# A product-key retrieval kernel: half of each chunk's second-table rows split into rounded halves, and the expert choice dealt out in finer steps

## The chip, the cores and the metric

The kernel runs on one core of a Trainium2 chip. The metric is the device time of one execution in microseconds. A core has five engines with a queue of instructions each: TensorE (PE, matmuls), VectorE (DVE), ScalarE (ACT), GpSimd (POOL) and SyncE (SP). An engine takes its instructions strictly in order and waits at one until what it needs has been signalled.

## The reference

One layer of a diffusion backbone over 640 tokens (128 context, 512 latent). The part that matters here is the channel mixer at its end, a retrieval over 16384 experts, each a row `u` of one table and a row `v` of another, both 2048 wide:

```python
top, sel = lax.top_k(cand, PEER_TOPK)          # 8 heads, 16 experts a head and token
idx = jnp.take_along_axis(cidx, sel, axis=-1)
g = jax.nn.softmax(top, axis=-1)
def block(args):                               # a block of 128 tokens
    xc, ic, gc = args
    act = jnp.einsum("cd,ckd->ck", xc, u_tab[ic])
    w = gc * jax.nn.gelu(act)
    return jnp.einsum("ck,ckd->cd", w, v_tab[ic])
```

`cand` are the sums of the 16 best scores of two key halves of 128 keys, so three kinds of top-16 are taken for each token and head.

## The kernel before

All stages up to the scores of the experts (modulation, mixers, projections) end about 2557 us into the span and are not touched. The rest is the function `experts`. It goes through five blocks of 128 tokens in the order 3, 4, 2, 1, 0. For each block a list of the experts that any of its tokens chose exists in HBM, and the block runs over this list in chunks of 256 experts. The first 24 chunks of a block (`K0`) are unconditional; further ones stand in nested `If`s on the length of the list.

A chunk (function `chunk`) fetches its 256 rows of `u` as two gathers of 128 rows, 1 MB each (`gather_u`, into `ur`), and turns them on TensorE in eight **turns** (`turn(g)`: four transposes of 128x128 into one of two PSUM tiles `tb`, a rounded copy `uh` by ScalarE, and the remainder `ul` by VectorE, whose row is named `wl<-tb,wh`). `up(g)` multiplies: three rounded (fp32r) products for each of two 128-blocks, xh*uh, xh*ul, xl*uh, into `a`. After `up(7)` ScalarE takes the GELU. The second half of a chunk's work is done while the next chunk turns, and the next chunk's code calls it `pending`: `up(7)`, then `weigh` (the GELU's result is transposed into a `tb` tile and multiplied by the gathered gates `gr` into `w`), then eight **downs** (`down(u)`, u = 4j + d: `w[:, j]` times 512 columns of `vr[j]`, in full fp32, summed into `acc[:, d]`). So one chunk's code is: turn 0, up 7 of before, turn 1, weigh, up 0, then for g = 2 to 7 turn g, down g-2, up g-1, and at the end downs 6 and 7.

The gathers are indirect DMAs that GpSimd issues, in the order in which the code calls them: the two halves of the next chunk's `u`, the gates (`gather_g`, two), two small gathers of list entries (`entries`), and the two halves of this chunk's `v` rows (`gather_v`, `vr[0]` after down 3, `vr[1]` after down 7 of before, since they overwrite what those read).

While a block runs, the experts of the next block are chosen (`choose`, a generator that `experts` steps once after each of the nine `yield`s of a chunk), mostly on VectorE: `top16` over 16 score rows of 128, sums `cand`, `top16` over 8 rows of 256, one-hot sums, then 32 rounds that build the gate table `Gs` by one-hot matmuls (`oh`, `dd`), and the list. The end of the block before (`finish`: gate, residual, layer norm, output) is a second generator, which is stepped at every other yield from chunk 1 on. The order of each engine's instructions in this stage is pinned to the order of the code (`pin`).

Of the kernel before, what the change touches and what calls it, by code (L numbers as in the profile page):

```python
# [7 lines left out]
F32 = mybir.dt.float32  # L8
F32R = mybir.dt.float32r
# [27 lines left out]
NCH = 64  # L37
# [114 lines left out]
class Kern:  # L152
# [871 lines left out]
                self.nc.vector.scalar_tensor_tensor(x[:, s], x[:, s], a, g, op0=o0, op1=o1)  # L1024

    def top16(self, vals, idx, src):
        v = self.nc.vector
        v.max(vals[:, 0:8], src)
        v.max_index(idx[:, 0:8], vals[:, 0:8], src)
        v.match_replace(src, vals[:, 0:8], src, -3.0e38)  # L1030
        v.max(vals[:, 8:16], src)
        v.max_index(idx[:, 8:16], vals[:, 8:16], src)

    def choose(self, b, S=None):
# [8 lines left out]
        IX = T.tile([128, 16, 16], U32, name="IX", tag="IX", bufs=1)  # L1043
        for c in range(16):
            self.top16(V[:, c], IX[:, c], S[:, c])
            if c % 2:
                yield
        IF = T.tile([128, 16, 16], F32, name="IF", tag="IF", bufs=1)
        v.tensor_copy(IF, IX)
        sh = [128, 8, 16, 16]  # L1050
# [3 lines left out]
        cand = T.tile(sh, F32, name="cand", tag="Gs", bufs=1)  # L1054
# [4 lines left out]
        TV = T.tile([128, 8, 16], F32, name="TV", tag="TV", bufs=1)  # L1059
        SE = T.tile([128, 8, 16], U32, name="SE", tag="SE", bufs=1)  # L1060
        for h in range(8):
            self.top16(TV[:, h], SE[:, h], cand[:, h].rearrange("p a b -> p (a b)"))
            yield

        I12 = T.tile([128, 3, 128], F32, name="I12", tag="I12", bufs=1)
# [36 lines left out]
        for n in range(34):  # L1102
            if full is not None:
                n1, p = full
                if n1 % 8 == 0:
                    st = T.tile([128, 128, 32], F32, name="Gs", tag="Gs", bufs=1)
                nc.scalar.copy(st[:, :, n1 % 8 * 4:n1 % 8 * 4 + 4], p.rearrange("j t i -> j i t"))
                if n1 % 8 == 7:
                    nc.sync.dma_start(self.G_d[b][:NE].rearrange("(i j) t -> j i t", j=128)
                                      [:, :, n1 // 8 * 32:n1 // 8 * 32 + 32], st)  # L1110
            full = None
            if ready is not None:
                n1, oh, dd = ready
                p = ps.tile([128, 4, 128], F32, name="g", tag="m", bufs=1)
                for j in range(4):
                    nc.tensor.matmul(p[:, j], oh[:, j], dd[:, j], start=True, stop=True)  # L1116
                full = n1, p
            ready = None
            if n < 32:
                oh = T.tile([128, 4, 128], F32, name="oh", tag="oa", bufs=2)  # L1120
                dd = T.tile([128, 4, 128], F32, name="dd", tag="od", bufs=2)
                for j in range(4):
                    k1, k2, w = (it[:, i, n * 4 + j:n * 4 + j + 1] for i in range(3))
                    v.tensor_scalar(oh[:, j], self.iota, k2, None, op0=ALU.is_equal)
                    v.tensor_scalar(dd[:, j], self.iota, k1, w, op0=ALU.is_equal, op1=ALU.mult)
                    if j == 1:
                        yield
                ready = n, oh, dd
            yield
            if n % 8 == 1 and n > 1:  # L1130
                for q in range(4):
                    v.tensor_reduce(cnt[:, n // 8 - 1, q * 32:q * 32 + 32], st[:, q * 32:q * 32 + 32], axis=AX.X,
                                    op=ALU.add)
                    yield

                for _ in range(20 if n < 32 else 0):
                    yield

        f = T.tile([128, 128], F32, name="f", tag="f", bufs=1)
        v.tensor_reduce(f, cnt.rearrange("p q i -> p i q"), axis=AX.X, op=ALU.add)  # L1140
# [7 lines left out]
        for r in range(16):  # L1148
            s = slice(r * 8, r * 8 + 8)
            v.max(L[:, s], f)  # L1150
            if r < 15:
                v.match_replace(f, L[:, s], f, 0.0)
            if r % 4 == 3:
                yield
        li = T.tile([128, 128], I32, name="li", tag="li", bufs=1)
        v.tensor_scalar(li, L, -1.0, None, op0=ALU.add)
# [86 lines left out]
    def up(self, g, x):  # L1243
# [5 lines left out]
        if g == 7:  # L1249
            self.nc.scalar.activation(self.t, self.a, AF.Gelu_apprx_tanh)  # L1250

    def weigh(self):

        p = self.bank()[:, :256].rearrange("p (j t) -> p j t", j=2)
        for j in range(2):
            self.nc.tensor.transpose(p[:, j], self.t[:, j * 128:j * 128 + 128], self.ident)  # L1256
        self.nc.vector.tensor_mul(self.w, p, self.gr)  # L1257

    def down(self, u, first):

        j, d = divmod(u, 4)
        self.nc.tensor.matmul(self.acc[:, d], self.w[:, j], self.vr[j][:, d * 512:d * 512 + 512],  # L1262
                              start=first and j == 0, stop=j == 1, skip_group_check=True)

    def chunk(self, i, c, pending, rows=None):


        nc, b = self.nc, self.order[i]
        self.nbank = 1
        x = self.xs[i % 2]  # L1270
        rows = rows or self.ur[c % 2]
        if c + 1 < NCH:
            self.gather_u(b, c + 1, 0)
        self.turn(0, rows)
        if pending is not None:
            first, before = pending
            self.up(7, before)
        self.turn(1, rows)
        yield
        if pending is not None:  # L1280
            self.weigh()
        self.gather_g(b, c)
        if c + 3 < NCH:
            self.entries(b, c + 3)
        self.up(0, x)
        yield
        if c + 1 < NCH:
            self.gather_u(b, c + 1, 1)
        for g in range(2, 8):
            self.turn(g, rows)  # L1290
            if pending is not None:
                self.down(g - 2, first)
                if g - 2 == 3:
                    self.gather_v(b, c, 0)
            self.up(g - 1, x)
            yield
        if pending is not None:
            self.down(6, first)
            self.down(7, first)
        else:  # L1300
            self.gather_v(b, c, 0)
        self.gather_v(b, c, 1)
        yield

# [69 lines left out]
    def experts(self):  # L1374
# [7 lines left out]
        self.ur = [[one([128, D], "ur%d%d" % (c, j)) for j in range(2)] for c in range(2)]  # L1382
        hb = self.H[GB]
        self.xs = [[t[:, j] for t in hb] for j in range(2)]
        first = [one([128, D], "uf%d" % j) for j in range(2)]
        pieces = [[t[:, k * 512:k * 512 + 512]
                   for t in [self.wp.tile([128, 1024], F32R, name=n, tag=n, bufs=self.hl_bufs) for _ in range(3)]
# [13 lines left out]
        for i, b in enumerate(self.order):  # L1401
            more = self.choose(self.order[i + 1]) if i < 4 else iter(())
            for c in range(K0):
                if c == 0 and i:
                    fin = self.finish(i - 1)
                    next(fin)
                for n, _ in enumerate(self.chunk(i, c, pending, rows)):
                    next(more, None)
                    if c and n % 2:
                        next(fin, None)  # L1410
                if c == 0:
                    next(fin, None)
                rows, pending = None, (c == 0, self.xs[i % 2])
                if c == 0 and i < 4:
                    self.load_x(i + 1)
            for _ in more:
                pass
            if i < 4:
                rows = first
# [13 lines left out]
            mark = self.pin()  # L1433
        self.nbank = 1
        self.up(7, pending[1])
        self.weigh()
        for u in range(8):
            self.down(u, False)
# [99 lines left out]
```

## Time and profile before

| what | us |
|---|---|
| median of 3 runs (5272.74 to 5280.17) | 5276.44 |
| the profiled execution's own time | 5268.44 |
| its span, first to last instruction | 5266.7 |

The profile is of one execution. Its times count from the span's start, so "at 4868.02" is a place in the program, and the 1.7 us between the span and that execution's own time lie around the program. The median of the timed runs is 8.0 us above the profiled execution.

### The profile page before, as it was taken

To read this page: it belongs to the slowest core of one execution; us is meant where nothing else is said; L and a number is where in the kernel's file an instruction comes from. 1 tells how busy PE (TensorE), PEld (TensorE's weight loads), DVE (VectorE), ACT (ScalarE), POOL (GpSimd) and SP (SyncE) were. 2 spreads that over 40 slices of the span, in tenths; PEclk is the share of its full clock that TensorE was granted. 3 is DMA by queue.
4 is the path that set the end of the run, shared out by engine and by line. 5 is a ranking of instruction groups with operands and counts; after the bars stand their busy time and mean duration, and the time that the engine had idled before them with its cause. 6 is when DMAs were issued, how large, how long until landed. Compare 5 with 4: busy or idle time off the path is not lost. (4 is left out here: it accounts for less than half of the span.)

```text
span 5266.7 us, 74372 instructions
## 1 busy us (share of the span) xinstructions
PE 4800.3 (91%) x29015; PEld 3989.4 (76%) x29015; DVE 2879.7 (55%) x6240; ACT 1599.6 (30%) x2561; POOL 1601.8 (30%) x1628
## 2 busy tenths in 40 slices
PE   8999989999999997969699979997999889989997
PEld 3799879999999977759577657765677667767775
DVE  6693593466534544781555566555655484634333
ACT  3324424433223123323133223322332223323222
POOL 2000493000000004534243434343334434344442
PEclk8999989999999998989799999999999999999998
DMA  6544336554325465563578768776777668867765
GB/s 238 195 173 144 126 129 213 192 173 172 114 98 165 147 214 200 158 153 136 187 242 257 233 221 272 244 235 240 254 242 243 255 218 267 247 231 290 260 250 212
DMA packets 576711, 1085.00 MB, mean 206 GB/s; under 512 B 375643, under 2 KB 388955, under 8 KB 501819
## 3 DMA queue, kind: packets, MB, share of 16 engines
q0 software_dynamic: 97712, 596.41, 30.5%
q1 hardware_dynamic: 460394, 429.32, 27.4%
q10 hardware_dynamic: 18208, 54.08, 2.6%
q8 instruction: 239, 3.92, 0.3%
q14 instruction: 158, 1.29, 0.1%
HBM read 967.53 MB, written 112.13 MB: 205 GB/s over the span
## 5 line engine op out<-in xcount | busy, mean ns | idle before, releaser
L1241 DVE TENSOR_TENSOR wl<-tb,wh 128x512 fp32r<-128x512 f32 x1072 | 738.0, 690 | 1368.1 <-ACT wh L1240 1366.7
L1240 ACT CAST wh<-tb 128x512 fp32r<-128x512 f32 x1072 | 627.5, 585 | 1873.2 <-PE tb L1239 1776.6
L1262 PE MATMUL acc<-vr,w 128*128 128x512 f32 x2144 | 1096.8, 604 | 30.3 <-DVE w L1257 30.1
L1248 PE MATMUL a<-wh,hh 128*128 128x256 f32 x2144 | 966.9, 451 | 1.8 <-PEq L1426 1.8
L1239 PE MATMUL tb<-cst,ur 128*128 128x128 f32 x4160 | 649.6, 279 | 68.1 <-DMA ur<-in_pu,ix 58.1
L1248 PE MATMUL a<-wl,hh 128*128 128x256 f32 x2144 | 618.8, 289 | 48.9 <-DVE wl L1241 48.7
L193 ACT CAST wh<-wr 128x1024 fp32r<-128x1024 f32 x339 | 355.5, 1050 | 983.4 <-PE a L630 380.4
L1248 PE MATMUL a<-wh,hl 128*128 128x256 f32 x2144 | 614.2, 286 | 0.0
L1248 PEld LDWEIGHTS a<-wl,hh 128*128 128x128 f32 x2144 | 419.9, 196 | 255.3 <-issue 170.5
L1239 PEld LDWEIGHTS tb<-cst,ur 128*128 128x128 f32 x4160 | 493.1, 143 | 150.9 <-issue 75.8
L1248 PEld LDWEIGHTS a<-wh,hh 128*128 128x128 f32 x2144 | 420.4, 196 | 199.4 <-issue 189.7
L630 PE MATMUL a<-h,wl 128*128 128x320 f32 x2368 | 550.9, 313 | 19.4 <-DVE wl L194 19.4
L1204 POOL DMA_INDIRECT vr<-in_pv,ix x268 | 256.1, 955 | 1015.5 <-PE acc L1262 909.8
L194 DVE TENSOR_TENSOR wl<-wr,wh 128x1024 fp32r<-128x1024 f32 x281 | 343.8, 1225 | 380.3 <-ACT wh L193 373.6
L630 PE MATMUL a<-h,wh 128*128 128x320 f32 x2368 | 549.0, 313 | 0.0
L630 PE MATMUL a<-l,wh 128*128 128x320 f32 x2368 | 545.9, 312 | 0.0
L1262 PEld LDWEIGHTS acc<-vr,w 128*128 128x128 f32 x2144 | 341.4, 194 | 103.9 <-issue 69.2
L630 PEld LDWEIGHTS a<-h,wl 128*128 128x128 f32 x2368 | 400.9, 190 | 21.7 <-DVE wl L194 21.0
L1248 PEld LDWEIGHTS a<-wh,hl 128*128 128x128 f32 x2144 | 416.2, 194 | 0.0
L630 PEld LDWEIGHTS a<-h,wh 128*128 128x128 f32 x2368 | 405.6, 190 | 12.0
L630 PEld LDWEIGHTS a<-l,wh 128*128 128x128 f32 x2368 | 400.9, 190 | 0.8
L1204 POOL DMA_INDIRECT gr<-G_d,ix x268 | 265.9, 992 | 365.4 <-DVE w L1257 280.9
(396 smaller groups left out, 7450.0 us busy)
## 6 DMA issues: line engine op xcount, KB each, us to landing
wr<-in_wmod SPq DMA_DIRECT2D x152, 512.0 KB
wr<-in_win SPq DMA_DIRECT2D x83, 512.0 KB
G_d<-Gs SPq DMA_DIRECT2D x20, 2048.0 KB
wrx<-in_win SPq DMA_DIRECT2D x69, 512.0 KB
wrx<-in_wmod SPq DMA_DIRECT2D x40, 512.0 KB
wr<-in_wo SPq DMA_DIRECT2D x36, 512.0 KB
wr<-in_wq SPq DMA_DIRECT2D x32, 512.0 KB
wrx<-in_wq SPq DMA_DIRECT2D x32, 512.0 KB
```

The lines of the kernel that those rows point to most:

```text
L193: nc.scalar.copy(h, raw)
L194: (eng or nc.vector).tensor_sub(l, raw, h.bitcast(F32))
L630: nc.tensor.matmul(a, w, x[:, kt, c0:c0 + n], start=kt == 0 and i == 0, stop=kt == nk - 1 and i == 2)
L1204: self.nc.gpsimd.indirect_dma_start(out=out, out_offset=None, in_=table, in_offset=bass.IndirectOffsetOnAxis(ap=idx, axis=0))
L1239: nc.tensor.transpose(p[:, k, j * 128:j * 128 + 128], rows[j][:, kt * 128:(kt + 1) * 128], self.ident)
L1240: nc.scalar.copy(self.uh[g % 4], p)
L1241: nc.vector.tensor_sub(self.ul[g % 4], p, self.uh[g % 4].bitcast(F32))
L1248: self.nc.tensor.matmul(self.a, a[:, kt], w[:, k], start=kt + n == 0, stop=kt == 15 and n == 2)
L1262: self.nc.tensor.matmul(self.acc[:, d], self.w[:, j], self.vr[j][:, d * 512:d * 512 + 512], start=first and j == 0, stop=j == 1, skip_grou ...
```

## The change

1. `down` for the first 128 experts of a chunk (j = 0) is no longer one fp32 product for each d but three rounded ones: Wh*vh, Wh*vl, Wl*vh. The downs of the second 128 experts stay as they are.
2. For this `vr[0]` is split in four pieces of 512 columns: `cast_v(d)` on ScalarE makes the rounded part `vh`, `rest_v(d)` on GpSimd subtracts it and makes `vl`. Pieces 0 and 1 stand in the first step of the next chunk (piece 0 ahead of up 7), pieces 2 and 3 with turns 2 and 3. `weigh` also makes `Wh` (ScalarE) and `Wl` (VectorE) from `w[:, 0]`.
3. The gathers move: both halves of the next chunk's `u` are called in the chunk's first step; the gates, the entries and `vr[0]` with turn 4; `vr[1]` stays at the end.
4. `choose` yields more often in its top-16 parts (16 and 16 steps in place of 8 and 8) and in the list (8 in place of 4); its 20 empty steps after every eighth round become 13, marked "idle". `finish` is stepped only when the choice is idle or over.

```diff
     def top16_steps(self, vals, idx, src):
         v = self.nc.vector
         v.max(vals[:, 0:8], src)
         v.max_index(idx[:, 0:8], vals[:, 0:8], src)
         v.match_replace(src, vals[:, 0:8], src, -3.0e38)
+        yield
         v.max(vals[:, 8:16], src)
         v.max_index(idx[:, 8:16], vals[:, 8:16], src)
...
         for c in range(16):
             self.top16(V[:, c], IX[:, c], S[:, c])
-            if c % 2:
-                yield
+            yield
...
-                for _ in range(20 if n < 32 else 0):
-                    yield
+                for _ in range(13 if n < 32 else 0):
+                    yield "idle"
...
+    def cast_v(self, d):
+
+        s = slice(d * 512, d * 512 + 512)
+        self.nc.scalar.copy(self.vh[:, s], self.vr[0][:, s])
+
+    def rest_v(self, d):
+        s = slice(d * 512, d * 512 + 512)
+        self.nc.gpsimd.tensor_sub(self.vl[:, s], self.vr[0][:, s], self.vh[:, s].bitcast(F32))
...
         self.nc.vector.tensor_mul(self.w, p, self.gr)
+        self.nc.scalar.copy(self.Wh, self.w[:, 0])
+        self.nc.vector.tensor_sub(self.Wl, self.w[:, 0], self.Wh.bitcast(F32))
...
-        self.nc.tensor.matmul(self.acc[:, d], self.w[:, j], self.vr[j][:, d * 512:d * 512 + 512],
-                              start=first and j == 0, stop=j == 1, skip_group_check=True)
+        s = slice(d * 512, d * 512 + 512)
+        for n, (w, x) in enumerate(((self.w[:, 1], self.vr[1][:, s]),) if j else
+                                   ((self.Wh, self.vh[:, s]), (self.Wh, self.vl[:, s]), (self.Wl, self.vh[:, s]))):
+            self.nc.tensor.matmul(self.acc[:, d], w, x, start=first and j == n == 0, stop=j == 1,
+                                  skip_group_check=True)
...
         if c + 1 < NCH:
             self.gather_u(b, c + 1, 0)
         self.turn(0, rows)
-        if pending is not None:
-            first, before = pending
+        if more:
+            self.cast_v(0)
+            self.rest_v(0)
             self.up(7, before)
...
         for g in range(2, 8):
             self.turn(g, rows)
-            if pending is not None:
+            if more:
+                if g < 4:
+                    self.cast_v(g)
+                    self.rest_v(g)
                 self.down(g - 2, first)
-                if g - 2 == 3:
-                    self.gather_v(b, c, 0)
+            if g == 4:
+                self.gather_g(b, c)
+                if c + 3 < NCH:
+                    self.entries(b, c + 3)
+                self.gather_v(b, c, 0)
             self.up(g - 1, x)
             yield
...
                 for n, _ in enumerate(self.chunk(i, c, pending, rows)):
-                    next(more, None)
-                    if c and n % 2:
+                    if next(more, "idle") == "idle" and c:
                         next(fin, None)
```

How the queues stand, first GpSimd's of one chunk (from the second half of a chunk's `v` rows on, in the first block). Before:

```order
L1204 DMA vr_22720<-in_pv,ix 128x2048
L1204 DMA ur_22725<-in_pu,ix 128x2048
L1204 DMA gr<-G_d_17687,ix 128x128 x2
L1204 DMA ix<-L_d_17692,si 128x1 x2
L1204 DMA ur_22726<-in_pu,ix 128x2048
L1204 DMA vr_22719<-in_pv,ix 128x2048
```

The same stretch with the change, where `hl` is the tile that `vl` lies in and `hh` that of `vh`:

```order
L1208 DMA vr_22720<-in_pv,ix 128x2048
L1208 DMA ur_22725<-in_pu,ix 128x2048
L1263 TENSOR_TENSOR hl<-vr_22719,hh 128x512
L1208 DMA ur_22726<-in_pu,ix 128x2048
L1263 TENSOR_TENSOR hl<-vr_22719,hh 128x512 x3
L1208 DMA gr<-G_d_17687,ix 128x128 x2
L1208 DMA ix<-L_d_17692,si 128x1 x2
L1208 DMA vr_22719<-in_pv,ix 128x2048
```

Four subtractions came in, the second `u` gather moved ahead of the four small gathers, and the gather of `vr[0]` now stands behind all of them.

ScalarE's queue from the casts of the last turn and turn 0 (`x2`) to those of turns 2 and 3, before:

```order
L1240 CAST wh<-tb_22743 128x512 x2
L1250 ACTIVATE t<-a 128x256
L1240 CAST wh<-tb_22744 128x512 x2
L1240 CAST wh<-tb_22743 128x512
L1240 CAST wh<-tb_22744 128x512
```

And with the change (`hh<-vr` is `cast_v`, `ACTIVATE t<-a` the GELU):

```order
L1244 CAST wh<-tb_22745 128x512 x2
L1259 CAST hh<-vr_22719 128x512
L1254 ACTIVATE t<-a 128x256
L1244 CAST wh<-tb_22746 128x512
L1259 CAST hh<-vr_22719 128x512
L1271 CAST Wh<-w 128x128
L1244 CAST wh<-tb_22746 128x512
L1259 CAST hh<-vr_22719 128x512
L1244 CAST wh<-tb_22745 128x512
L1259 CAST hh<-vr_22719 128x512
```

The first `cast_v` stands ahead of the GELU, and `Wh` ahead of the cast of turn 2.

VectorE's queue in the first steps of a choice, before: between two remainders `wl` of turns stand two whole top-16s.

```order
L1241 TENSOR_TENSOR wl<-tb_22744,wh 128x512
L1028 MAX V<-S 128x8
L1029 MAX_INDEX IX<-V,S 128x8
L1030 MATCH_REPLACE S<-V,S 128x128
L1031 MAX V<-S 128x8
L1032 MAX_INDEX IX<-V,S 128x8
L1028 MAX V<-S 128x8
L1029 MAX_INDEX IX<-V,S 128x8
L1030 MATCH_REPLACE S<-V,S 128x128
L1031 MAX V<-S 128x8
L1032 MAX_INDEX IX<-V,S 128x8
```

With the change, from the remainder of turn 1 over `weigh` to that of turn 2:

```order
L1245 TENSOR_TENSOR wl<-tb_22746,wh 128x512
L1032 MAX V<-S 128x8
L1033 MAX_INDEX IX<-V,S 128x8
L1034 MATCH_REPLACE S<-V,S 128x128
L1036 MAX V<-S 128x8
L1037 MAX_INDEX IX<-V,S 128x8
L1270 TENSOR_TENSOR w<-tb_22745,gr 128x256
L1272 TENSOR_TENSOR Wl<-w,Wh 128x128
L1032 MAX V<-S 128x8
L1033 MAX_INDEX IX<-V,S 128x8
L1034 MATCH_REPLACE S<-V,S 128x128
L1036 MAX V<-S 128x8
```

One top-16 stands in a step, and `Wl`, which waits for ScalarE's `Wh`, stands behind `w`.

## Rows read from the trace of the kernel before

**Rows 1.** The page's costliest groups, the downs' line (count | busy, mean ns).

```profile
L1262 PE MATMUL acc<-vr,w 128*128 128x512 f32 x2144 | 1096.8, 604 | 30.3 <-DVE w L1257 30.1 <-DMA vr<-in_pv,ix 0.2
```

**Rows 2.** Windows: stretch, its length, each engine's busy time, granted clock, DMA share, GB/s.

```profile
2557.50:4723.80 2166.30, 1944.61 (x11350) 1471.64 (x11350) 1249.37 (x3213) 617.16 (x1106) 841.30 (x868) 0.96 0.73 242
4723.80:5266.70 542.90, 497.50 (x2866) 366.93 (x2866) 198.93 (x316) 151.37 (x267) 221.16 (x232) 0.97 0.68 250
3091.40:3200.80 109.40, 80.35 (x404) 57.59 (x403) 98.62 (x289) 25.55 (x42) 35.46 (x33) 0.88 0.59 207
4802.00:5193.70 391.70, 383.62 (x2254) 285.37 (x2255) 134.84 (x207) 116.57 (x208) 174.63 (x185) 1.00 0.70 258
4395.60:4415.90 20.30, 20.04 (x132) 15.97 (x131) 12.61 (x41) 6.61 (x13) 7.65 (x8) 1.00 0.56 197
```

**Rows 3.** Windows of line L1256 alone (weigh's transposes, two a chunk).

```profile
2557.50:4723.80 2166.30, 46.67 (x208) 23.98 (x208) 0.96 0.73 242
4802.00:5193.70 391.70, 9.41 (x46) 4.60 (x47) 1.00 0.70 258
```

**Rows 4.** The longest wait of PE from 2557 us on: total, times, longest.

```profile
PE tb L1256 <- DVE wl L1241: 93.0, 106, 6.2
```

**Rows 5.** Timeline of PE across a chunk's start in the last block (start, duration).

```profile
4866.30 1.88 PE L1262 MATMUL acc<-vr,w 128*128 128x512 f32 x4
...
4868.02 0.60 PE L1239 MATMUL tb<-cst,ur 128*128 128x128 f32 x4
...
4870.11 0.41 PE L1256 MATMUL tb<-cst,t 128*128 128x128 f32 x2 [0.34 <-DVE wl L1241]
...
4871.73 1.02 PE L1262 MATMUL acc<-vr,w 128*128 128x512 f32 x2
...
4873.73 0.60 PE L1262 MATMUL acc<-vr,w 128*128 128x512 f32 x1
```

**Rows 6.** Timelines of ACT and DVE at the same place.

```profile
4869.37 0.38 ACT L1250 ACTIVATE t<-a 128x256 f32<-128x256 f32 x1
4870.49 0.69 DVE L1241 TENSOR_TENSOR wl<-tb,wh 128x512 fp32r<-128x512 f32 x1 [0.52 <-ACT wh L1240]
4871.10 0.41 DVE L1257 TENSOR_TENSOR w<-tb,gr 128x256 f32<-128x256 f32 x1
```

**Rows 7.** Timeline of POOL around there.

```profile
4862.00 0.95 POOL L1204 DMA_INDIRECT vr<-in_pv,ix  x1 [1.28 <-PE acc L1262]
...
4873.04 0.96 POOL L1204 DMA_INDIRECT gr<-G_d,ix  x1 [0.30 <-issue]
```

**Rows 8.** DMA issues and median us to landing: 4851 to 4853 us, then 4800 to 5200.

```profile
vr<-in_pv,ix POOLq DMA_INDIRECT x1, 5.2
...
vr<-in_pv,ix POOLq DMA_INDIRECT x47, 5.8
```

**Rows 9.** Window of the fp32r products of 512 columns in an earlier stage (L957).

```profile
2149.70:2159.70 10.00, 10.00 (x45) 8.04 (x44) 1.00 0.56 190
```

**Rows 10.** Sources L301 and L198: duration ns min/median/max.

```profile
L301 POOL TENSOR_TENSOR x<-x,xp x16: 1282/1292/2382, 1905.8 to 2163.1; 128x512 f32<-128x512 f32 x16
...
L198 ACT CAST hh<-mm x20: 611/618/622, 2018.5 to 2386.7; 128x512 fp32r<-128x512 f32 x20
```

**Rows 11.** Timeline of DVE beside the slowest of L301 on POOL.

```profile
2157.38 3.46 DVE L1076 TENSOR_TENSOR oh<-oa,cst 128x1024 f32<-128x1024 f32 x2
```

**Rows 12.** Timeline of DVE, the first instructions of two top-16s in a row.

```profile
3092.91 0.28 DVE L1028 MAX8 V<-S 128x8 f32<-128x128 f32 x1
...
3094.62 0.27 DVE L1028 MAX8 V<-S 128x8 f32<-128x128 f32 x1
```

**Rows 13.** Timeline of PE, and two windows (as rows 2): clock after idle time.

```profile
3180.47 0.41 PE L1256 MATMUL tb<-cst,t 128*128 128x128 f32 x2 [1.97 <-DVE wl L1241]
...
3181.70:3185.10 3.40, 3.19 (x9) 1.76 (x8) 3.37 (x6) 0.58 (x1) 2.15 (x2) 0.50 0.86 316
4213.00:4217.00 4.00, 2.58 (x9) 1.28 (x9) 3.73 (x18) 0.00 (x0) 0.23 (x1) 1.00 0.00 0
```

More of the change, by code (lines that the diff above doesn't have):

```diff
@@ L1026, in top16, with top16_steps @@
     def top16(self, vals, idx, src):
+        for _ in self.top16_steps(vals, idx, src):
+            pass
+    def top16_steps(self, vals, idx, src):
         v = self.nc.vector
@@ L1061, in choose @@
         for h in range(8):
-            self.top16(TV[:, h], SE[:, h], cand[:, h].rearrange("p a b -> p (a b)"))
+            yield from self.top16_steps(TV[:, h], SE[:, h], cand[:, h].rearrange("p a b -> p (a b)"))
             yield
@@ L1152, in choose @@
                 v.match_replace(f, L[:, s], f, 0.0)
-            if r % 4 == 3:
+            if r % 2:
                 yield
@@ L1271, in chunk @@
         rows = rows or self.ur[c % 2]
+        more = pending is not None
+        first, before = pending or (None, None)
         if c + 1 < NCH:
@@ L1274, in chunk @@
         self.turn(0, rows)
-        if pending is not None:
-            first, before = pending
+        if more:
+            self.cast_v(0)
+            self.rest_v(0)
             self.up(7, before)
+        if c + 1 < NCH:
+            self.gather_u(b, c + 1, 1)
         self.turn(1, rows)
+        if more:
+            self.cast_v(1)
+            self.rest_v(1)
         yield
-        if pending is not None:
+        if more:
             self.weigh()
-        self.gather_g(b, c)
-        if c + 3 < NCH:
-            self.entries(b, c + 3)
         self.up(0, x)
         yield
-        if c + 1 < NCH:
-            self.gather_u(b, c + 1, 1)
         for g in range(2, 8):
             self.turn(g, rows)
-            if pending is not None:
+            if more:
+                if g < 4:
+                    self.cast_v(g)
+                    self.rest_v(g)
                 self.down(g - 2, first)
-                if g - 2 == 3:
-                    self.gather_v(b, c, 0)
+            if g == 4:
[3 more added lines that the diff above has]
+                self.gather_v(b, c, 0)
             self.up(g - 1, x)
             yield
-        if pending is not None:
+        if more:
             self.down(6, first)
             self.down(7, first)
-        else:
-            self.gather_v(b, c, 0)
         self.gather_v(b, c, 1)
@@ L1384, in experts @@
         self.xs = [[t[:, j] for t in hb] for j in range(2)]
+        self.vh, self.vl = (t[:, 2].rearrange("p k t -> p (k t)") for t in hb)
+        self.Wh, self.Wl = (one([128, 128], n, F32R) for n in ("Wh", "Wl"))
         first = [one([128, D], "uf%d" % j) for j in range(2)]
@@ L1416, in experts @@
             for _ in more:
+                pass
+            for _ in fin:
                 pass
@@ L1435, in experts @@
         self.up(7, pending[1])
+        for d in range(4):
+            self.cast_v(d)
+            self.rest_v(d)
         self.weigh()
```

## The prediction

> **What bounds the kernel now.** I read the trace by stages first. The windows put 2166 us on the first four blocks and 543 us on the last [rows 2], and the count of weigh's transposes, two for each chunk, says 104 of them in the first four blocks (with the very first chunk, that has none, 105 chunks: 20.6 us each, 541.6 us a block) and 23 in the stretch 4802 to 5194 [rows 3]. That stretch has no choice in it, and gives the undisturbed chunk: 391.7 / 23 = 17.03 us, PE busy in 383.6 of 391.7 us, the clock at 1.00 [rows 2]. So there TensorE is the bound. A block with a choice pays 3.6 us more a chunk, and the next rows say for what. In the first 109 us of a choice VectorE is busy in 98.6 and TensorE in only 80.4, the clock at 0.88: VectorE is the bound, and the longest wait of TensorE is the one for its remainders `wl` [rows 2, 4]. In the rounds TensorE is full again (20.04 of 20.30 us): there the one-hot matmuls come on top [rows 2].
>
> **The products.** The trace has 2144 down records, two for one fp32 product, so 1072 products in 134 chunks [rows 1]. Two downs take from 4866.30 to 4868.02, so one takes 0.86 us [rows 5]. An fp32r product of 512 columns is in the trace of an earlier stage: 45 records touch 10.00 us, two of them cut by its ends, so 0.23 us each [rows 9]. Three take 0.70. A chunk saves 4 x 0.16 = 0.64 us, 86 us over the kernel if TensorE stayed the bound everywhere.
>
> **What is put in front of them.** ScalarE gets four casts (0.62 us, the row from SBUF [rows 10]) and `Wh` (128 columns; estimated at 0.3, below the 0.38 of the GELU's 256 columns [rows 6]). GpSimd gets four subtractions; its nearest row is the addition of 128x512 at 1.29 us when nothing disturbs it [rows 10]. VectorE gets `Wl`, about 0.25. None of these engines is full, but all three are in order, and the first cast stands ahead of the GELU, on which weigh, and with it TensorE's whole queue, waits.
>
> So I followed one undisturbed chunk from the end E of its first `cast_v`. The GELU takes 0.38, the cast of turn 1 0.6, its remainder 0.69 and `w` 0.41 [rows 6], which with 0.05 between engines ends at E+2.2. `Wh` is ready at E+2.5, and down 0 starts. It takes 0.70; up 1 and turn 3 take 2.00 - 0.86 = 1.14 (two downs stand 2.00 apart, one of them in it [rows 5]): E+4.4. The cast of turn 3 starts 0.25 later and ends at E+5.2, the fourth `cast_v` at E+5.85, the fourth subtraction at E+7.15. Behind it on GpSimd stand the four small gathers, which issue 1.26 us apart [rows 7], so `vr[0]` is issued at E+12.2. One such gather that was issued with none in flight landed after 5.2 us; the median is 5.8 [rows 8]. I take 5.4, nearer the first, since little is in flight at that place: E+17.6. Then the next chunk's first cast takes 0.62: **18.2 us** from one E to the next. Before, `vr[0]` was issued at 4862.00, 6.0 us ahead of turn 0, and was needed by down 0, 3.7 us behind turn 0 [rows 5, 7]. Now it is issued about 3 us ahead of turn 0 and needed 1.2 us behind it. The saving on TensorE doesn't matter in this ring: what it does itself in a chunk (17.03 less 0.64, and some 0.7 for weigh and down 0, which now wait for longer queues on ScalarE) is about 17.1 us, so it waits a further 1.1 us at weigh, about 1.9 us in one piece with the waits that are there.
>
> Two more costs hang on that. First, the port. While an addition on GpSimd took 2.38 us instead of 1.29, VectorE's one-hot products, with both operands in SBUF, took 3.46 us for two [rows 10, 11]; the two hold each other up. `Wl` has both operands in SBUF and is due at E+2.5, where the second subtraction runs (E+2.3 to E+3.6). The wait is between 0 (if `Wl` comes first) and 1.05; down 0's third product, turn 3 and so the ring wait with it. I take 0.5, since the two are due within 0.2 us of each other. The Trainium skill, "SBUF — State Buffer", section "Who interferes with whom", says that a VectorE instruction with two SBUF inputs and a GpSimd one that reads SBUF exclude each other for a whole instruction, the first to start winning. The rows agree; taken at its full length the rule makes 0.8 us more of this place, 54 us over the 68 undisturbed chunks.
>
> Second, the clock. After an idle time of 1.97 us the granted clock fell to 0.50, the lower of its two levels (1.2 GHz), for 3.40 us; in a stretch with 2.58 of 4.00 us busy it stayed at 1.00 [rows 13]. An idle time of 1.9 stands between. Where it falls, down 0, up 1 and turn 3 take up to 1.4 us longer. Bounds 0 and 1.4; I take 0.4, three chunks in ten. Undisturbed chunk with the change: 18.2 + 0.5 + 0.4 = **19.1 us** (18.0 to 20.6).
>
> **The choice.** One 128-wide top-16 takes 1.71 us [rows 12]. Before, two stood in a step, 4.1 us with a remainder, against 2.0 us of TensorE. Now one does: 2.4 us against 1.84. VectorE remains the bound in these 16 steps, but over 2 chunks: 27.4 + 2 x 6.5 (eight remainders, `w`, `Wl`, one wait) and about 6 for the sums and the first products of `finish`, 47 us. The next 31 steps (halves of the 256-wide, one-hots) are 3.4 chunks; a step of some 1.2 us stands ahead of `w`, so the ring is longer there, 19.8 us: 68 us. The 82 steps of the rounds are 9.1 chunks; TensorE's 20.30 less 0.64, and 1.0 for the longer chain: 20.7, 188 us. The list's 18 steps are 2 chunks at 20.3, and six more small gathers of 1.26 us stand in GpSimd's queue: 48 us. The idle steps (39 in the rounds, 28 at the end) and the chunks past the 24th make 9.7 undisturbed chunks: 185 us. `finish` lies in them and is hidden, since VectorE has some 11 us free in each (134.8 busy of 391.7 us in 23 chunks [rows 2]). Without that cover it would cost what it costs now in the first chunks.
>
> **Sum.** 47 + 68 + 188 + 48 + 185 = 536 us for a block, against 541.6: 4 x -5.6 = -22 us. In the last block 29 chunks x (19.1 - 17.03) = +60, and 4 us behind it for the last subtractions. Together +42 on the profiled execution's own 5268.4. That one is 8 us below the median of the runs: forecast **5318**, 0.8% slower; its own range is 5285 to 5380.
>
> **Rivals.**
> (a) `vr[0]` comes in time. The ring closes below TensorE's 17.1 if landing takes 4.3 us; that decides. Then undisturbed chunks take 17.3 and the others lose a part of their wait: a block 509 us, the last +12, in all -118: 5158. For it: the ring is only 1.1 us too long, and four terms of it are from other places. Against it: the shortest landing that I have a row for is 5.2 us. The Trainium skill, "DMA: Bandwidth & Descriptors", section "Anatomy of one DMA — SWDGE (gpsimd) path", gives 2.0 us plus the bytes at 436 GB/s, an estimate of 4.4 us for 1 MB, and so this case; the rows, 5.2 to 5.8, are above it.
> (b) The ring holds, but port and clock cost nothing: 18.2 us undisturbed, a block 523.5, the last +38, in all -34: 5242. For it: 1.9 us is less than the 1.97 after which the clock fell.
> (c) Both cost in full: 20.6 us; a block 565, the last +108, in all +200: 5478. For it: each fall of the clock lengthens the next wait.
>
> **Numbers.** Forecast 0.45, (a) 0.15, (b) 0.27, (c) 0.13. A measurement here tells about 0.2%, 10.5 us, from no change. Case (b) is spread over some 30 us, two thirds of it faster, a quarter the same. So faster 0.32, same 0.10, slower 0.58. The range leaves out (a) and the upper part of (c): 5215 to 5440.
>
> **What would show it.** In the last block: chunks of 18 to 20 us in place of 17.03; ScalarE waiting for the landing of `vr`, weigh's transposes waiting for the GELU; `vr[0]` issued about 12 us behind the first `cast_v`; the clock below 1.00 in part of the chunks. Of the products: three of 0.23 us apart. Of the choice: the stretch in which VectorE is full covers two chunks of some 23 us each. I am wrong if undisturbed chunks are at 17 us or below, or if GpSimd's subtraction is well off 1.29 us.

## The result, and the profile after

The changed kernel takes 5671.72 us (5663.17 to 5680.77, 4 runs) against 5275.76 us: **1.075 times as long, 95% interval 1.073 to 1.077**. Forecast were 5318 us and a range of 5215 to 5440. The direction was right; the size was not: the profiled span is 5677.6 us long, 410.9 more than before, where the sum said 42.

Windows as in [rows 2]: 18 undisturbed chunks of the last block, one chunk of them, and the one behind it; then 16 chunks of one choice, from the one-hot sums through the rounds; then the first two chunks of that choice.

```profile
5111.00:5489.10 378.10, 315.79 (x1837) 251.06 (x1837) 148.70 (x180) 132.18 (x253) 229.09 (x217) 0.95 0.58 207
5198.30:5219.10 20.80, 16.63 (x102) 13.11 (x102) 8.74 (x10) 7.32 (x15) 12.70 (x13) 1.00 0.59 210
5219.10:5237.90 18.80, 16.63 (x103) 13.20 (x103) 6.16 (x10) 7.42 (x15) 12.78 (x13) 1.00 0.64 229
...
3255.50:3643.70 388.20, 319.07 (x1895) 265.70 (x1895) 252.39 (x522) 137.84 (x264) 210.11 (x193) 0.89 0.69 217
3168.80:3214.20 45.40, 38.01 (x205) 30.05 (x205) 41.85 (x155) 14.90 (x30) 26.97 (x25) 0.87 0.49 171
```

And of weigh's transposes alone, as in [rows 3]:

```profile
3255.50:3643.70 388.20, 8.03 (x32) 3.89 (x32) 0.89 0.69 217
5111.00:5489.10 378.10, 7.90 (x37) 3.66 (x37) 0.95 0.58 207
```

An undisturbed chunk takes 378.1 / 18 = 21.0 us (before 17.03, forecast 19.1). Two kinds of chunk stand side by side: in one VectorE is busy for 8.74 us, in the next, 2.0 us shorter, for 6.16. In the third stretch a chunk takes 388.2 / 16 = 24.3 us. It holds 27 steps of the one-hot part, 80 of the rounds and 38 idle ones; by the forecast's prices 3.0 x 19.8 + 8.9 x 20.7 + 4.2 x 19.1 = 324 us, 20.1 a chunk. The first two chunks of a choice take 45.4 us; 47 were forecast.

The longest waits of TensorE from 2557 us on (as [rows 4]), and ScalarE's for the gather:

```profile
PE tb L1269 <- ACT t L1254: 256.7, 116, 10.1
PE acc L1280 <- DVE Wl L1272: 96.1, 57, 2.6
PE g L1120 <- ACT Gs L1111: 91.5, 41, 6.8
PE acc L1280 <- ACT Wh L1271: 47.0, 48, 4.9
...
ACT hh L1259 <- DMA vr<-in_pv,ix: 207.5, 103, 9.6
```

The first is the ring that was foreseen: weigh waits for the GELU, which stands behind `cast_v(0)`, which waits for `vr[0]`. In a chunk without other trouble (timelines of ScalarE and GpSimd):

```profile
5218.18 0.62 ACT L1259 CAST hh<-vr 128x512 fp32r<-128x512 f32 x1 [1.45 <-DMA vr<-in_pv,ix]
...
5236.91 0.62 ACT L1259 CAST hh<-vr 128x512 fp32r<-128x512 f32 x1 [1.18 <-DMA vr<-in_pv,ix]
...
5222.47 3.77 POOL L1263 TENSOR_TENSOR hl<-vr,hh 128x512 fp32r<-128x512 f32 x3
5226.40 0.97 POOL L1208 DMA_INDIRECT gr<-G_d,ix  x1 [0.16 <-issue]
...
5231.45 0.95 POOL L1208 DMA_INDIRECT vr<-in_pv,ix  x1 [0.30 <-issue]
```

From the end of one first cast (5218.80) `vr[0]` is issued 12.65 us later and lands 5.46 us after that; the next cast ends at 5237.53: 18.7 us around, 18.2 were worked out. The second wait is the one that was taken as 0.5 us. Timelines of VectorE and GpSimd in the chunk before, where `Wl` fell among subtractions, and then in this one, where it did not:

```profile
5200.16 2.96 DVE L1272 TENSOR_TENSOR Wl<-w,Wh 128x128 fp32r<-128x128 f32 x1 [0.36 <-ACT Wh L1271]
...
5220.98 0.29 DVE L1272 TENSOR_TENSOR Wl<-w,Wh 128x128 fp32r<-128x128 f32 x1 [0.36 <-ACT Wh L1271]
...
5199.49 0.96 POOL L1208 DMA_INDIRECT ur<-in_pu,ix  x1
5200.47 2.49 POOL L1263 TENSOR_TENSOR hl<-vr,hh 128x512 fp32r<-128x512 f32 x2
```

In the first chunk `Wl` fell due at 5200.16, ahead of both subtractions, while GpSimd still issued the gather of `ur` (5199.49 to 5200.45). It ended at 5203.12, 0.16 us after the second of two subtractions in a row: 2.96 us in place of 0.29, 2.67 us late. In 15 of the 18 chunks `Wl` takes 1.75 us or more, in 14 of them 2.96 or more, which agrees with VectorE's extra busy time, 148.70 - 18 x 6.16 = 38 us.

The hold did not always last over the whole row. Here, in a chunk of the first choice, `Wl` fell due when the first of two subtractions was already running, and it ended at 2629.99, some 0.15 us after that one (2628.55 + 1.29), although the second followed at once (VectorE, then GpSimd):

```profile
2628.73 1.26 DVE L1272 TENSOR_TENSOR Wl<-w,Wh 128x128 fp32r<-128x128 f32 x1 [0.36 <-ACT Wh L1271]
...
2628.55 2.59 POOL L1263 TENSOR_TENSOR hl<-vr,hh 128x512 fp32r<-128x512 f32 x2
```

The third wait was not in the prediction at all. One place in the rounds, of VectorE, GpSimd, ScalarE and TensorE:

```profile
3571.80 2.04 DVE L1128 TENSOR_SCALAR oh<-cst,itT 128x128 f32<-128x128 f32 x1
...
3574.01 0.41 DVE L1270 TENSOR_TENSOR w<-tb,gr 128x256 f32<-128x256 f32 x1
...
3571.47 0.98 POOL L1208 DMA_INDIRECT ur<-in_pu,ix  x1
3572.47 1.28 POOL L1263 TENSOR_TENSOR hl<-vr,hh 128x512 fp32r<-128x512 f32 x1
...
3574.46 0.30 ACT L1271 CAST Wh<-w 128x128 fp32r<-128x128 f32 x1 [3.23 <-DVE w L1270]
3574.66 0.58 ACT L1111 COPY Gs<-g 128x512 f32<-128x512 f32 x1
...
3575.29 2.08 PE L1120 MATMUL g<-dd,oh 128*128 128x128 f32 x8 [3.87 <-ACT Gs L1111]
```

A one-hot instruction of the choice, 0.28 us long elsewhere, takes 2.04 us beside a gather's issue and a subtraction on GpSimd; `w` stands behind it, `Wh` on ScalarE waits 3.23 us for `w`, the copy of `Gs` stands behind `Wh`, and TensorE waits 3.87 us for the copy. The eight matmuls then take 2.08 us; the granted clock is at 0.50, the lower of its two levels, from 3575.2 to 3577.4.

### The profile page after: what moved, and what is told of

Its sections match the earlier page's. It is cut to its first block, busy times and chain, and to the rows that moved or that the text cites. A ratio compares the mean times of both kernels' runs of the same rounds, so it can differ in the third digit from the quotient of the medians.

```text
span 5677.6 us, 76797 instructions
## 1 busy us (share of the span) xinstructions
PE 4893.6 (86%) x29551; PEld 4219.1 (74%) x29551; DVE 3177.6 (56%) x6374; ACT 1899.1 (33%) x3231; POOL 2301.6 (41%) x2164
## 4 chain that ended last, share of the span: by engine, by line
POOL 15%; DMA 12%; issue 10%; PE 9%; DVE 6%; ACT 3%; POOLq 0%; ACTq 0%; DVEq 0%
DMA vr<-in_pv,ix 10%; POOL hl L1263 6%; POOL ix L1208 3%; POOL gr L1208 3%; PE acc L1280 3%; PE a L1252 2%; PE tb L1243 2%; PE g L1120 2%; DMA ix<-L_d,si 1%; POOL ur L1208 1%; ACT hh L1259 1%; ACT wh L1244 1%; DVE wl L1245 1%; DVE oh L1128 1%; DVE Wl L1272 1%
## 5 line engine op out<-in xcount | busy, mean ns | idle before, releaser
L1263 POOL TENSOR_TENSOR hl<-vr,hh 128x512 fp32r<-128x512 f32 x536 | 685.2, 1286 | 612.0 <-ACT hh L1259 607.2
L1252 PE MATMUL a<-wh,hh 128*128 128x256 f32 x2144 | 766.8, 358 | 4.5 <-issue 4.5
L1243 PE MATMUL tb<-cst,ur 128*128 128x128 f32 x4160 | 681.3, 290 | 32.6 <-DMA ur<-in_pu,ix 29.0
L1252 PE MATMUL a<-wh,hl 128*128 128x256 f32 x2144 | 633.0, 295 | 0.0
L1243 PEld LDWEIGHTS tb<-cst,ur 128*128 128x128 f32 x4160 | 524.7, 149 | 103.1 <-issue 78.5
L1280 PE MATMUL acc<-vr,w 128*128 128x512 f32 x1072 | 526.2, 593 | 0.0
L1252 PEld LDWEIGHTS a<-wl,hh 128*128 128x128 f32 x2144 | 438.8, 205 | 102.9 <-issue 45.0
L1252 PEld LDWEIGHTS a<-wh,hh 128*128 128x128 f32 x2144 | 440.7, 206 | 93.9 <-issue 68.9
L1252 PEld LDWEIGHTS a<-wh,hl 128*128 128x128 f32 x2144 | 437.4, 204 | 0.0
L1259 ACT CAST hh<-vr 128x512 fp32r<-128x512 f32 x536 | 334.2, 624 | 207.5 <-DMA vr<-in_pv,ix 207.5
```

The source lines that it names most:

```text
L1243: nc.tensor.transpose(p[:, k, j * 128:j * 128 + 128], rows[j][:, kt * 128:(kt + 1) * 128], self.ident)
L1252: self.nc.tensor.matmul(self.a, a[:, kt], w[:, k], start=kt + n == 0, stop=kt == 15 and n == 2)
L1259: self.nc.scalar.copy(self.vh[:, s], self.vr[0][:, s])
L1263: self.nc.gpsimd.tensor_sub(self.vl[:, s], self.vr[0][:, s], self.vh[:, s].bitcast(F32))
L1280: self.nc.tensor.matmul(self.acc[:, d], w, x, start=first and j == n == 0, stop=j == 1, skip_group_check=True)
```

## The experiments

Ratios are to the kernel before on the same chip, with 95% intervals.

**The two parts apart.** `choice_alone` is the kernel before with point 4 of the change, `split_alone` the changed kernel without it.

> The kernel before with the finer and even steps of the choice alone (and the end of a block stepped in the idle steps); products, gathers and queues as before. Theory A (the loss of the change is all in the split and its queues): the first two chunks of a choice took 37.5 and 30.5 us before and 25.2 and 20.2 us with the change, so this part alone gains 20 to 25 us a block and up to that again from the list and the idle steps: 5180 to 5230 us. Rival B (the work on VectorE is only moved, into chunks that pay for it there): 5260 to 5290 us.

> The changed kernel with the old, coarse steps of the choice: split, three products and moved gathers alone. Theory A (the two parts add): the changed kernel's 5672 plus the 40 to 100 us that the finer steps bring, 5710 to 5770 us. Rival B (the finer steps hurt the split, since they put work of the choice ahead of w and Wl in the queues in every step): 5560 to 5650 us.

Measured: 0.988 (0.987 to 0.990) and 1.087 (1.085 to 1.088); 0.988 x 1.087 = 1.074, so the parts add. The choice gains 1.2%, at the weak end of what theory A said. `finish`, now packed into the idle steps, waits for its rows (timeline of VectorE, here for 6.40 us):

```profile
3259.44 0.75 DVE L1335 SCALAR_TENSOR_TENSOR wr<-wr,bmv,wh 128x512 f32<-128x512 f32 x1 [6.40 <-DMA wh<-in_lnr]
```

That this costs time is not shown: these waits of VectorE add up to 40.5 us in `choice_alone` and to 43.9 in `choice_paced` below, which stepped `finish` half as often and took the same time.

The split with its gathers costs 8.7%, and the next runs take it apart.

**Ring and port.** `v_first` calls the gather of `vr[0]` ahead of the four small ones; `wl_psum` leaves `w` of the first 128 experts in PSUM, so that the subtraction of `Wl` has one operand there; `psum_vfirst` does both.

```diff
             if g == 4:
+                self.gather_v(b, c, 0)
                 self.gather_g(b, c)
                 if c + 3 < NCH:
                     self.entries(b, c + 3)
-                self.gather_v(b, c, 0)
...
-        self.nc.vector.tensor_mul(self.w, p, self.gr)
-        self.nc.scalar.copy(self.Wh, self.w[:, 0])
-        self.nc.vector.tensor_sub(self.Wl, self.w[:, 0], self.Wh.bitcast(F32))
+        self.nc.vector.tensor_mul(p[:, 0], p[:, 0], self.gr[:, 0])
+        self.nc.scalar.copy(self.Wh, p[:, 0])
+        self.nc.vector.tensor_mul(self.w[:, 1], p[:, 1], self.gr[:, 1])
+        self.nc.vector.tensor_sub(self.Wl, p[:, 0], self.Wh.bitcast(F32))
```

> The changed kernel, with w of the first 128 experts left in PSUM, so that the subtraction that makes Wl has one operand in SBUF in place of two; nothing else. Theory port (Wl is held up by two subtractions of GpSimd in a row, 2.2 us in most chunks): Wl takes its 0.25 us, undisturbed chunks fall from 21.2 to about 18.7 us, that of the ring, and 134 chunks give 5330 to 5430 us. Rival ring (the wait at Wl only fills slack that the late first half of the v rows leaves): 5600 to 5670 us.

> The changed kernel, with the gather of vr[0] issued ahead of the gates and the list entries with turn 4, 5 us earlier; nothing else. Theory ring: the first cast no longer waits for the gather, the ring closes below TensorE's own time, and what is left over 17.1 us is the 2.3 us of the port: about 19.5 us a chunk, 5400 to 5500 us. Rival port (the lock alone sets the chunk, and the ring is behind it): 5620 to 5680 us.

> The changed kernel with both edits: vr[0] gathered ahead of the gates and entries, and w of the first 128 experts left in PSUM for Wl. The undisturbed chunk was 17.15 us with the early gather alone, so nothing is left there for the second edit. Theory port: in the chunks of a choice TensorE still waited 52 us for Wl, with the clock behind it some 80: 5360 to 5410 us. Rival (in those chunks VectorE is held at the choice's own instructions instead, and Wl only shows it): 5430 to 5465 us.

Measured: `wl_psum` 1.049 (1.047 to 1.051), between the two expectations; `v_first` 1.033 (1.032 to 1.035), in the ring theory's range; `psum_vfirst` 1.014 (1.013 to 1.016), with 5353 us just below the port theory's range. Undisturbed chunks, first of `wl_psum` (20 chunks, then two of them), then of `v_first` (19 chunks):

```profile
5066.60:5447.70 381.10, 339.53 (x2040) 277.40 (x2040) 124.52 (x220) 145.76 (x280) 254.79 (x240) 0.95 0.65 228
5105.60:5123.80 18.20, 16.27 (x102) 13.11 (x102) 6.23 (x11) 7.30 (x15) 12.75 (x13) 1.00 0.68 240
5123.80:5143.40 19.60, 17.68 (x102) 14.58 (x102) 6.23 (x11) 7.31 (x15) 12.75 (x13) 0.91 0.63 222
```

```profile
5058.20:5384.00 325.80, 315.31 (x1939) 250.24 (x1939) 116.95 (x190) 137.61 (x267) 241.32 (x229) 1.00 0.72 253
```

Without the hold of `Wl` the ring alone gives 19.06 us: 18.2 in chunks at full clock, as worked out, and 19.6 where it fell to 0.91. With the early gather the ring is gone, the clock stays at 1.00, and a chunk takes 17.15 us. Here the ring theory's account failed, though its total came out: it left the port's 2.3 us in the undisturbed chunk, 19.5 us. `Wl` is not held there any more, as VectorE's busy time tells: 116.95 / 19 = 6.16 us a chunk. So the hold in the undisturbed chunks came with the ring's timing, and the total was met because the chunks of a choice cost more.

TensorE is now busy for 315.31 of 325.80 us, yet a chunk is no shorter than before, although each down of the first half is shorter. PE of `v_first`, the transposes of turns 3 to 5 and one product between them:

```profile
5147.23 0.60 PE L1243 MATMUL tb<-cst,ur 128*128 128x128 f32 x4
...
5148.22 0.50 PE L1280 MATMUL acc<-hl,Wh 128*128 128x512 f32 x1 [0.16 <-POOL hl L1263]
...
5149.50 0.60 PE L1243 MATMUL tb<-cst,ur 128*128 128x128 f32 x4
...
5151.35 0.60 PE L1243 MATMUL tb<-cst,ur 128*128 128x128 f32 x4
```

The step from turn 4 to turn 5 takes 1.85 us, against 2.00 before [rows 5]: the 0.15 us that was worked out. The step ahead of it takes 2.27, because the pieces come late (the second product waits for `hl`). The gain and the lateness cancel.

**Four additions alone.** `four_adds` is the kernel before with four additions of 128x512 on GpSimd in each chunk, behind the issue of `vr[0]`, on tiles that nothing else uses.

```diff
                 if g - 2 == 3:
                     self.gather_v(b, c, 0)
+                    for d in range(4):
+                        s = slice(d * 512, d * 512 + 512)
+                        nc.gpsimd.tensor_add(self.o2[:, s], self.o1[:, s].bitcast(F32), self.o1[:, s].bitcast(F32))
```

> The kernel before, with four additions of 128x512 on GpSimd added to each chunk, one behind the other, between the gathers of vr[0] and vr[1]; nobody reads their result. Theory port: the undisturbed chunk, in which no VectorE instruction has all its inputs in SBUF, stays at 17.03 us; in the chunks of a choice the one-hot instructions, whose one tensor is in SBUF, are held for as long as the additions run, 2 to 5 us in some 15 chunks of each of four blocks, partly hidden: 5320 to 5420 us. Rival (only instructions with two inputs in SBUF are held): 5270 to 5300 us.

Measured: 1.022 (1.021 to 1.024), as the port theory said. Undisturbed chunks stay at 170.2 / 10 = 17.0 us; a one-hot instruction of the choice, whose only tensor operand is in SBUF, is held until the last of the additions is done (VectorE, then GpSimd, then the window of 10 chunks):

```profile
3249.28 4.76 DVE L1125 TENSOR_SCALAR dd<-cst,itT 128x128 f32<-128x128 f32 x1
...
3248.95 0.95 POOL L1204 DMA_INDIRECT vr<-in_pv,ix  x1 [2.38 <-PE acc L1262]
3249.91 4.03 POOL L1297 TENSOR_TENSOR hl<-hh 128x512 fp32r<-128x512 f32 x4
...
5017.30:5187.50 170.20, 166.70 (x980) 123.95 (x981) 58.63 (x90) 50.78 (x91) 116.48 (x121) 1.00 0.69 255
```

The Trainium skill, "SBUF — State Buffer", section "Who interferes with whom", names `tensor_scalar` among the operations that can contend with GpSimd, under conditions that it gives, and lets the one that starts first keep the port for a whole instruction. The run agrees on the operation. On who wins it differs, and the measurement decides: the one-hot instruction started 0.63 us ahead of the first addition, while GpSimd issued a gather, and yet it was held, for 4.76 us, over four instructions in a row.

**Off ScalarE, off GpSimd.** On top of `v_first`, `sub_dve` makes the four subtractions on VectorE. On top of `psum_vfirst`, `wh_dve` makes `Wh` on VectorE; `all_dve` then makes the subtractions there too, the first two behind `Wl`.

```diff
-        self.nc.scalar.copy(self.Wh, p[:, 0])
+        self.nc.vector.tensor_copy(self.Wh, p[:, 0])
...
-        self.nc.gpsimd.tensor_sub(self.vl[:, s], self.vr[0][:, s], self.vh[:, s].bitcast(F32))
+        self.nc.vector.tensor_sub(self.vl[:, s], self.vr[0][:, s], self.vh[:, s].bitcast(F32))
```

> The changed kernel with the early gather of vr[0], and with the four subtractions that make vl on VectorE in place of GpSimd, so that GpSimd computes nothing in this stage. Theory port (GpSimd's subtractions hold VectorE up, the choice's one-hot instructions as well as Wl, and through w, Wh and the copy of Gs they hold TensorE): the waits of TensorE for Gs (85 us), Wh (67) and Wl (52) fall to a quarter, with the clock that they cost 5220 to 5330 us. Rival (VectorE, which gets some 2.7 us more work in a chunk, is late by as much in the chunks of a choice): 5400 to 5520 us.

> As the kernel with both edits (early gather, w in PSUM), and Wh made by VectorE in place of ScalarE, so that nothing on ScalarE waits for w; the subtractions stay on GpSimd. Theory queue (the copy of Gs is late because it stands behind Wh, which waits for w, which waits for the choice's work on VectorE): the waits for Gs fall from 85 us to under 30, and the time by 60 to 120 us against the kernel with both edits: 5260 to 5340 us. Rival (w itself is late, and TensorE waits at the first product for it whoever makes Wh): within 30 us of the kernel with both edits.

> The changed kernel with the early gather of vr[0], w in PSUM, Wh made by VectorE, and the four subtractions on VectorE too, the first two of them behind w, Wh and Wl (and the second and third product of a down exchanged to fit): GpSimd computes nothing. Theory port (what is left over the finer choice alone, 1.6 points, is GpSimd holding the choice's own instructions): 0.985 to 0.997 of the kernel before, 5200 to 5262 us where that takes 5277. Rival (VectorE has too much to do in the chunks of a choice, 2.7 us more in each): 1.002 to 1.020.

Measured: `sub_dve` 1.014 (1.013 to 1.016), between the two expectations and level with `psum_vfirst`: the wait for `Wl` is gone, but that for `Wh` (first row below) rose from 66.7 us in `v_first`; two subtractions stand ahead of `w` on VectorE now. `wh_dve` 1.004 (1.003 to 1.006): TensorE's wait for `Gs` fell from 82.2 us in `psum_vfirst` to 31.7 (second row) and the time by 56 us, both just short of what the queue theory said (under 30, and 60 to 120).

```profile
PE acc L1280 <- ACT Wh L1271: 117.9, 101, 6.2
```

```profile
PE g L1120 <- ACT Gs L1111: 31.7, 43, 1.8
```

`all_dve` 1.001 (1.000 to 1.002): a little better again, and between the expectations. With the ring open, GpSimd without subtractions and `Wh` off ScalarE, the split makes the kernel no faster than before; against `choice_alone` it still costs 1.3 points. Waits are left: TensorE's for the GELU, which stands behind `cast_v(0)`, adds up to 87.3 us (about 10 in `choice_alone`). In the undisturbed chunks little is lost, 308.70 / 18 = 17.15 us against 17.03; so most of the 1.3 points lies in the chunks of a choice.

```profile
PE tb L1269 <- ACT t L1254: 87.3, 106, 9.2
```

```profile
4858.70:5167.40 308.70, 299.76 (x1836) 237.22 (x1837) 157.19 (x288) 124.98 (x235) 137.23 (x145) 1.00 0.72 253
```

**A split that starts early.** `early_split` gathers `vr[0]` with turn 2, splits two pieces with turn 7 and behind it, and two with turns 0 and 1 of the next chunk; `w` in PSUM, `Wh` on VectorE, `finish` at every other idle step.

> The changed kernel, re-staged so that nothing waits for the split: vr[0] gathered with turn 2, its pieces 0 and 1 split with turn 7 and behind it, pieces 2 and 3 with turns 0 and 1 of the next chunk behind the GELU, w of the first 128 experts in PSUM, Wh made by VectorE, and the end of a block paced at every other idle step. Theory (the products' 0.64 us a chunk are real and were eaten by waits): undisturbed chunks of 16.4 to 16.6 us, 5080 to 5160 us, the fastest of all. Rival port (GpSimd's subtractions hold the choice's instructions wherever they stand): undisturbed chunks as said, but those of a choice 2 us above the paced kernel's, 5180 to 5280 us.

Measured: 1.028 (1.026 to 1.029), against both. On GpSimd the issues of four gathers of 1 MB now begin within 6.3 us; these are the first and the last, and the cast that needs the last starts 10.8 us later, at 5321.93 (5.46 in the changed kernel), having waited 4.45 us for it; subtractions, the next gathers, the cast of turn 0 and the GELU stand behind it.

```profile
5304.93 0.96 POOL L1208 DMA_INDIRECT vr<-in_pv,ix  x1
...
5311.15 0.96 POOL L1208 DMA_INDIRECT vr<-in_pv,ix  x1 [0.27 <-POOL hl L1263]
```

**The gathers, and a faster version.** `gathers_alone` is the kernel before with its gathers moved as in point 3. `choice_paced` is `choice_alone` with `finish` at every other idle step, `paced_u` that with the second `u` gather in the first step. `u_entries` is `choice_alone` with the second `u` gather and the two list entries in the first step, the gates where they were.

```diff
+        if c + 1 < NCH:
+            self.gather_u(b, c + 1, 1)
+        if c + 3 < NCH:
+            self.entries(b, c + 3)
         self.turn(1, rows)
...
         self.gather_g(b, c)
-        if c + 3 < NCH:
-            self.entries(b, c + 3)
         self.up(0, x)
         yield
-        if c + 1 < NCH:
-            self.gather_u(b, c + 1, 1)
```

> The kernel before with the moved gathers alone: both halves of the next chunk's u in the first step, the gates and the list entries ahead of vr[0] (which stays behind down 3, since down 3 still reads it). Theory ring (the gathers' places cost nothing as long as the v rows are not split): undisturbed chunks stay at 17.03 us, and the chunks that waited for the second u gather gain, 5235 to 5280 us. Rival (the order of the gathers costs by itself, vr[0] lands late behind four small ones): undisturbed chunks above 17.5 us, 5320 to 5400 us.

> The finer steps of the choice on the kernel before, as in the first run of that part, but with the end of the block before stepped at every other idle step in place of every one. In that run VectorE waited 6.4, 2.5 and 1.3 us for rows of the layer norm in one chunk of each block (27 and 25 to 30 us with the clock behind it). Theory (these waits are the pace's): they go, 10 to 15 us a block, 5150 to 5190 us. Rival (they come back at the block's end, where the steps that are left run together): 5205 to 5245 us.

> The same, and the second u gather of the next chunk issued in the chunk's first step. Theory: the waits of TensorE for u rows (some 14 us outside the very first one, and their clock) go: 10 to 30 us less than the paced kernel. Rival: within 8 us of it, since the u rows that are late are those of a block's end, where the list bounds them.

> The finer choice on the kernel before, with the second u gather in the chunk's first step, followed by the two list entries; the gates' gathers, which wait for w, behind them. Theory row (casts of ScalarE start late when seven gathers are issued without a pause; here it is five, then a pause): undisturbed chunks of 17.03 us, 0.980 to 0.989 of the kernel before. Rival (two u gathers and the second half of v in flight together do it, whatever stands behind them): undisturbed chunks of 18.0 to 18.4 us, 0.997 to 1.003.

Measured: `gathers_alone` 1.012 (1.010 to 1.013), its rival; `choice_paced` 0.989 (0.988 to 0.991), the same as `choice_alone`, so its rival too; `paced_u` 1.001 (1.000 to 1.002), worse than either expectation; `u_entries` **0.982 (0.980 to 0.983)**, the fastest of all, faster than both kernels. Undisturbed chunks are 383.9 / 21 = 18.3 us in `gathers_alone` and 425.6 / 25 = 17.0 us in `u_entries` (windows below). In `gathers_alone` ScalarE's casts of turns 3 to 5 start late: by the trace, which models the ends of matmuls, turn 4's transposes end at 5215.04; its cast starts at 5217.62, and what ended its wait was TensorE's signal.

```profile
4916.80:5300.70 383.90, 361.94 (x2058) 259.92 (x2058) 121.14 (x189) 104.39 (x190) 159.66 (x169) 1.00 0.65 238
...
5214.44 0.60 PE L1239 MATMUL tb<-cst,ur 128*128 128x128 f32 x4
...
5217.62 1.07 ACT L1240 CAST wh<-tb 128x512 fp32r<-128x512 f32 x2 [2.99 <-PE tb L1239]
```

```profile
4694.40:5120.00 425.60, 416.80 (x2451) 309.94 (x2451) 146.65 (x225) 126.87 (x226) 190.49 (x201) 1.00 0.71 257
...
5067.25 0.95 POOL L1208 DMA_INDIRECT vr<-in_pv,ix  x1 [5.49 <-PE acc L1266]
...
5074.79 0.96 POOL L1208 DMA_INDIRECT gr<-G_d,ix  x1 [0.30 <-issue]
```

`u_entries` came out as its theory said, and yet refutes the reason: its seven gathers, too, are issued without a pause (5067.25 to 5074.79), and no cast is late. `paced_u` has the long chunk, too, 329.1 / 18 = 18.3 us; but for the pace of `finish`, which cost nothing in `choice_paced`, it differs from `u_entries` only in that the gates are gathered ahead of the entries. So the order of the gathers decides it, not their number in a row; what delays the casts stays open. In the changed kernel, whose subtractions stand between them, the delay was not seen.

## Why the prediction was wrong

- **Products: right.** 0.15 us a down where nothing waits; a chunk without the ring takes 17.15 us where "about 17.1" was said for TensorE itself.
- **Ring: right.** 18.2 said, 18.7 seen in the changed kernel and 18.2 in `wl_psum`; `v_first` shows that it is the late `vr[0]`. Casts (0.62), subtractions (1.29), `Wh` (0.30) and landing (5.46) were as taken.
- **Port: the step that failed.** "The wait is between 0 (if `Wl` comes first) and 1.05" took the hold to end with the subtraction at work, and to be nothing for a `Wl` that comes first. `Wl` did come first, by 0.31 us, while a gather was issued, and was held over both subtractions behind it: 2.67 us in 14 of 18 chunks, 21.0 - 19.06 = 1.9 us a chunk with what follows, where 0.5 was taken. (The 0.8 us more that the forecast names beside this price is a whole subtraction less 0.5; it goes beyond the forecast's own bound of 1.05 and is still too small.)
- **Clock: mis-sized.** A fall cost the 1.4 us that were said (19.6 against 18.2 in `wl_psum`), but it came in 11 of the 20 chunks of `wl_psum`, not in three of ten: 19.06 - 18.2 = 0.9 us a chunk where 0.4 were taken.
- **Rounds: a wait that was not there in the sum.** 20.7 us a chunk came from TensorE and a longer chain. The port was asked about for `Wl` alone; but the choice's one-hot instructions are held too, and `w`, `Wh` and the copy of `Gs` stand behind them in two in-order queues. `wh_dve` takes one link of this chain away and gains 1.0 point against `psum_vfirst`.
- **Sizes.** The profiled execution is 369 us above the sum. If the four choices are alike, the third stretch makes 4 x (388 - 324) = 256 of it; the undisturbed chunks outside of it, 29 and four times 5.4, make 50.6 x (21.0 - 19.1) = 96. How the 256 divide among the hold of `Wl`, the chain of the rounds and the clock is not measured.
- **Choice: right in kind.** 45.4 us for two chunks against 47; alone it gains 1.2%.
- **Rivals.** (c) was the nearest, but its full price of the port, 1.05 us, was the same mistake. (b), which put port and clock at nothing, was wrong on both. (a) is what `v_first` makes true by hand, and undisturbed chunks then take 17.15 us, where (a) said 17.3; but (a)'s total, 5158 us or 0.978, is far from `v_first`'s 1.033, where TensorE still waits 84.9 us for `Gs`, 66.7 for `Wh` and 52.4 for `Wl`.

What is open: why `all_dve` stays 1.3 points above `choice_alone`, most of it in the chunks of a choice. VectorE's added work would fit, and so would the four casts on ScalarE, of which the first stands ahead of the GELU; neither was tried by itself. Open is also what lets `Wl` in between two subtractions when the first is already running: in `v_first` a one-hot instruction in the same position, at 2854.91, took 2.43 us, over both.

## What to carry to other kernels

Before work is moved to GpSimd, list every VectorE instruction that can fall beside it, not only the new one, and price the hold by the whole row of GpSimd's instructions that follow one another without a pause, the longest that was seen here, then by what stands behind the held one in each in-order queue. A transfer whose issue is moved behind work that depends on its own landing closes a ring; work out the ring's length beside the engines' loads, since the longer of the two is the stage's time (here 18.2 us against 17.15). A gain of 0.15 us in some steps is worth nothing if the operands of the others come as much too late.

## What the runs showed of the hardware

- A VectorE instruction that fell due while GpSimd issued a gather was held over all the GpSimd instructions that followed without a pause: 4.76 us beside four additions of 1.0 us, 2.96 us beside two subtractions of 1.25 us. One that fell due with the first of two subtractions running took 1.26 us and ended with that one.
- Held were a `tensor_scalar` with its one tensor operand in SBUF (`four_adds`) and a subtraction with both operands there; the same subtraction with one operand in PSUM was not held in `wl_psum` (0.28 us, all 134 times).
- The granted clock was 0.91 over a chunk with 1.88 us of idle time at weigh (19.6 us, at 5123.80 in `wl_psum`), and 1.00 over the one before it with 1.95 us (18.2).
- Four 1 MB gathers whose issues began within 6.3 us: the last was there 10.8 us after its own issue, against 5.46 in the changed kernel.
- In `gathers_alone` a cast on ScalarE started 2.6 us after the modelled end of the transposes that it reads, and chunks took 18.3 us in place of 17.0; no cause was found.
